# Unnormalised FFN inputs, an output projection traced in one go, and SSD running sums spread over the partitions by transfers

## The chip, the cores and the metric

The kernel runs on one core of a Trainium2 chip. The metric is the device time of one execution in microseconds (us); below, "before" is the kernel as it stood and "after" is the changed one. The core's engines are PE (TensorE, matrix multiply), DVE (VectorE), ACT (ScalarE), POOL (GpSimd) and SP (SyncE, which here only issues transfers). Each engine runs its own instructions in the order in which they stand in its program, and waits on semaphores for the others.

## The reference

Two layers of a hybrid decoder over a prompt of 512 tokens and eight sequences of eight new tokens each. Per layer:

```python
h = rmsnorm(x); u, z, xbc, dt, cq, ckv, kpe = split(h @ w_in)
y = concat(pool_mix(u), ssd_mix(z, xbc, dt), mla_mix(cq, ckv, kpe)) @ w_out
x = x + y
x = x + (relu(rmsnorm(x) @ w_up) ** 2) @ w_down     # rmsnorm: x * rsqrt(mean(x*x) + eps) * g
```

The SSD part takes chunks of 128 tokens. With `a = dt * A` per token and head, `a_cs = cumsum(a)` along the chunk, it needs the matrix `L[l, s] = exp(a_cs[l] - a_cs[s])` for s <= l, and `exp(a_cs[l])` for what comes in from the chunk before. One last rmsnorm gives the outputs.

## The kernel before

Activations lie transposed: 128 channels on the partitions, tokens along the free dimension. The tokens are worked on in two groups, c = 0 (256 prompt tokens) and c = 1 (256 prompt tokens and the 64 new ones, so 320 columns). Names carry layer, group and number: `out017` is the output projection of layer 0, group 1, output tile 7; `dn0033` is the down projection of layer 0, group 0, part 3, tile 3; `in102` is the input projection of layer 1, group 0, tile 2.

Every float32 product of a projection is three products of rounded parts (lines 201 to 203): weights and activations are split into a high part (`wh`, `gh`) and a low part (`wl`, `gl`). A weight tile comes in two halves of 256 KB (`wr`, line 177, issued by SP into four buffers); ACT makes `wh` (L191) and DVE `wl` (L192), in three buffers each, and a half feeds 12 matmuls. Results go to PSUM banks of tag `mm`, of which there are two.

The streams of work (input projection, SSD, attention over the prompt, attention of the new tokens, output projection, and the FFN of the other group) are generators, and a `Weave` takes steps from them in turn by rates. That gives the order in which instructions are traced, which is their priority. A scheduler of the framework then makes each engine's order from priorities and modelled times, so a change of a few lines moves instructions far from it.

Three places of this kernel matter here.

The input of the FFN: after the eight tiles of `w_out`, the sum of squares `ssf` is turned into `r` = rsqrt(mean) by a matmul with ones, then Ln and Exp on ACT (`rstd_of`). Then per tile DVE makes `fn` = x * g * r (L963), ACT the high part (L964), DVE the low part (L965). The splits are stored in the buffers that held the mixer's outputs, so they can begin once the last tile of `w_out` has read these. Only in layer 1, group 1 are the splits made without `r` (`late_norm`), and `r` is multiplied in after the up projection (L1016); elsewhere ACT applies Relu there (L1018).

The SSD's sums: `a` is split in two parts (`ah`, L816, L817) and per chunk b and head group g six matmuls with a column of it spread over all 128 columns put the running sums into a PSUM tile `rb` (L856), three heads side by side on every partition. ACT takes the exponential of it for `Ez` (L860), DVE adds the causal mask into `rm` (L863), ACT takes exp (L867), DVE multiplies by `cb` (L870), and PE uses it for `y` (L880). `rm` has two buffers.

The end: `finish_y` multiplies the eight tiles by r, two of them on POOL (L1030), and sends them out in pairs (L1032).

Of the kernel before, what the change touches and what calls it, by code (L numbers as in the profile page):

```python
# [9 lines left out]
F32 = mybir.dt.float32  # L10
F32R = mybir.dt.float32r
# [78 lines left out]
def step_kernel(ctx: ExitStack, tc: tile.TileContext, I, O):  # L90
# [121 lines left out]
    def rstd_of(c, ssum, n, name, tag):  # L212
# [6 lines left out]
        r = ap.tile([P, CM], F32, tag=tag, name=f"r_{name}", bufs=2)[:, :cw]  # L219
# [134 lines left out]
    def mixer(l, c, mp, ep):  # L354
# [252 lines left out]
        def sample_attn():  # L607
# [48 lines left out]
            ol = tr[0].tile([P, 6, NSEQ, DSEQ], F32, tag="ol", name=f"ol{l}{c}")  # L656
            for pq_ in range(NSEQ // 2):
# [72 lines left out]
                done.add(f"s{2 * pq_ + 1}")  # L730
                V.tensor_copy(ol[:, :, 2 * pq_:2 * pq_ + 2], po[:, :P].rearrange("p (u h t) -> p h u t", u=2, t=DSEQ)[:, :6])
# [36 lines left out]
        def ssd_dt():  # L768
# [46 lines left out]
            ah = mp.tile([P, 2, 18], F32R, tag="ah", name=f"ah{l}{c}")  # L815
            V.tensor_copy(ah[:, 0], a)  # L816
            V.tensor_tensor(ah[:, 1], a, ah[:, 0].bitcast(F32), op=ALU.subtract)  # L817
# [11 lines left out]
            st['dt'] = dt, ah, ncs, dec, tot  # L829
            yield 0.5  # L830

        def ssd():
            dt, ah, ncs, dec, tot = st['dt']
            for b in range(3 if smp_c else 2):
# [15 lines left out]
                for g in range(2):  # L850
                    r64 = slice(64 * g, 64 * g + 64)
                    rb = psum('sc', f"rb{l}{c}{b}{g}")
                    for r in range(3):
                        h = 3 * g + r
                        for i in range(2):
                            T.matmul(rb[:, r * n:r * n + n], ah[:n, i, 6 * b + h:6 * b + h + 1].broadcast_to([n, P]),  # L856
                                     CR('US')[:n] if smp else CR('U'), start=(i == 0), stop=(i == 1))
                    if not first:
                        ez = Ez[r64, g, :, :n]
                        A.activation(ez, rb[r64, :3 * n].rearrange("p (r k) -> p r k", r=3), AF.Exp)  # L860
                        V.tensor_tensor(ez, bc(xa[r64, 4, off:off + n], 3), ez, op=ALU.mult)
                    rm = mp.tile([P, 3, P], F32, tag="rm", name=f"rm{l}{c}{b}{g}", bufs=2)
                    V.tensor_tensor(rm[:n, :, :n], rb[:n, :3 * n].rearrange("p (r k) -> p r k", r=3),  # L863
                                    bc(C('mssds')[:n] if smp else C('mssd'), 3), op=ALU.add)
# [68 lines left out]
        def w_out():  # L933
# [6 lines left out]
            xu = []  # L940
            late_norm = l == DEPTH - 1 and c == 1
            for m in range(KT):
# [5 lines left out]
                if late_norm:  # L948
                    xu.append(t)
                sq_acc(c, ssf, t, m == 0, f"f{l}{c}{m}")  # L950
                yield 3.3
            if late_norm:
                ff[c] = act_tiles(c, f"f{l}{c}")
                for m in range(KT):
                    scaled_split(xu[m], ff[c], m, par(l, 'ffn_g', m))
                rf[0] = rstd_of(c, ssf, D, f"f{l}{c}", "rstd")
                return
            r = rstd_of(c, ssf, D, f"f{l}{c}", "rstd")
            ff[c] = act_tiles(c, f"f{l}{c}")
            for m in range(KT):  # L960
                pl, w_, tag, bufs = (ep, cw, "fn", 3) if c == 0 else (tr[0], 512, "ku", NK)
                t = pl.tile([P, w_], F32, tag=tag, name=f"fn{l}{c}{m}", bufs=bufs)[:, :cw]
# [38 lines left out]
    rf = [None]  # L1001
    NG, GT = 4, 8

    def ffn(l, c, fp, beside):
# [5 lines left out]
        def up(g, j):  # L1010
# [275 lines left out]
```

## Time and profile before

| | us |
|---|---|
| three runs, median (lowest to highest) | 1461.06 (1459.27 to 1461.63) |
| the profiled execution's own time | 1453.98 |
| its span, first to last instruction | 1452.2 |
| PE busy in it | 1405.4 (97%) |
| DVE busy | 1063.3 (73%) |
| ACT busy | 843.6 (58%) |

The profiled execution is one of the quicker ones: its own time lies 7.08 us under the median of the runs. A busy share is an average over the whole span. Where PE has work without a gap, time is the number of matmuls by their spacing; what the other engines do costs time only where PE waits for it. A matmul's own duration (some 0.3 us) is longer than its spacing, since matmuls are pipelined.

### The profile page before, as it was taken

Reading aid. Unit: us, or ns where it says so; the run is one execution under the profiler, and the core shown is the slowest. Engines: PE = TensorE matmul, PEld = TensorE weight load, DVE = VectorE, ACT = ScalarE, POOL = GpSimd, SP = SyncE. Lnnn points to the kernel's source line nnn. Section 1 sums busy time; section 2 is a strip of 40 time slices with the busy share of each in tenths; the row PEclk is TensorE's granted clock in tenths of the full one; section 3 lists DMA queues with packets and bytes.
Section 4 is the critical chain, followed back from the end, with each engine's and each line's share of the span. In section 5 each row is a group of like instructions: output and inputs, shape, how many; then the busy total and the mean of one; then the engine's idle time right before and its main releaser. Section 6 shows DMA issues by size and latency. Waiting matters only on the chain.

```text
span 1452.2 us, 30116 instructions
## 1 busy us (share of the span) xinstructions
PE 1405.4 (97%) x10552; PEld 1344.1 (93%) x10552; DVE 1063.3 (73%) x2353; ACT 843.6 (58%) x1781; POOL 74.7 (5%) x182
## 2 busy tenths in 40 slices
PE   7998989999999979999999999999999999999997
PEld 7968968999999979889999999899999999999997
DVE  6979769777666779856676679977777668675765
ACT  7756536665665657655454556656656666443444
POOL 0021013000000001100000001310000000000000
PEclk9999989999999999999999999999999999999999
DMA  7423416667545634434544553555675455444442
GB/s 230 132 70 123 142 41 210 196 205 239 161 144 177 201 114 141 139 103 154 162 151 154 167 165 122 157 195 168 209 233 169 130 175 170 151 151 148 153 150 105
DMA packets 152425, 228.95 MB, mean 158 GB/s; under 512 B 17874, under 2 KB 61010, under 8 KB 152274
## 3 DMA queue, kind: packets, MB, share of 16 engines
q1 hardware_dynamic: 138610, 216.69, 46.8%
q10 hardware_dynamic: 13664, 10.34, 2.3%
q8 instruction: 83, 1.36, 0.4%
q14 instruction: 68, 0.56, 0.1%
HBM read 219.32 MB, written 7.64 MB: 156 GB/s over the span
## 4 chain that ended last, share of the span: by engine, by line
PE 89%; DVE 5%; DMA 2%; ACT 2%; issue 1%; SPq 0%; ACTq 0%; DVEq 0%
PE dn L203 9%; PE dn L201 9%; PE dn L202 9%; PE up L203 9%; PE up L202 9%; PE up L201 9%; PE in L201 4%; PE in L203 4%; PE in L202 4%; PE out L201 2%; PE out L203 2%; PE out L202 2%; PE spo L726 2%; PE o L601 2%; PE rb L856 1%
## 5 line engine op out<-in xcount | busy, mean ns | idle before, releaser
L201 PE MATMUL up<-gh_f,wh_up 128*128 128x256 f32 (+1 forms) x1024 | 305.4, 299 | 1.8 <-ACT gh_f L238 1.1
L203 PE MATMUL up<-gh_f,wl_up 128*128 128x256 f32 (+1 forms) x1024 | 306.0, 300 | 0.1
L202 PE MATMUL up<-gl_f,wh_up 128*128 128x256 f32 (+1 forms) x1024 | 305.1, 298 | 0.3 <-DVE gl_f L239 0.3
L203 PE MATMUL dn<-hh,wl_dn 128*128 128x256 f32 (+1 forms) x1024 | 304.3, 298 | 0.6 <-DVE wl_dn L192 0.6
L201 PE MATMUL dn<-hh,wh_dn 128*128 128x256 f32 (+1 forms) x1024 | 303.4, 296 | 0.0
L202 PE MATMUL dn<-hl,wh_dn 128*128 128x256 f32 (+1 forms) x1024 | 303.0, 296 | 0.0
L191 ACT ACTIVATE wh_dn<-wr_dn 128x512 fp32r<-128x512 f32 x256 | 160.8, 631 | 185.7 <-PE dn L202 130.5
L191 ACT ACTIVATE wh_up<-wr_up 128x512 fp32r<-128x512 f32 x256 | 160.7, 629 | 165.7 <-PE up L202 108.4
L192 DVE TENSOR_TENSOR wl_dn<-wr_dn,wh_dn 128x512 fp32r<-128x512 f32 x256 | 176.4, 691 | 84.1 <-ACT wh_dn L191 76.8
L192 DVE TENSOR_TENSOR wl_up<-wr_up,wh_up 128x512 fp32r<-128x512 f32 x256 | 177.6, 696 | 63.1 <-ACT wh_up L191 55.3
L201 PEld LDWEIGHTS up<-gh_f,wh_up 128*128 128x128 f32 x1024 | 193.6, 189 | 4.2 <-ACT gh_f L238 1.3
L203 PEld LDWEIGHTS up<-gh_f,wl_up 128*128 128x128 f32 x1024 | 193.3, 189 | 4.6 <-DVE wl_up L192 1.6
L202 PEld LDWEIGHTS up<-gl_f,wh_up 128*128 128x128 f32 x1024 | 193.7, 189 | 1.9 <-issue 0.7
L203 PEld LDWEIGHTS dn<-hh,wl_dn 128*128 128x128 f32 x1024 | 192.8, 188 | 2.2 <-DVE wl_dn L192 1.0
L201 PEld LDWEIGHTS dn<-hh,wh_dn 128*128 128x128 f32 x1024 | 192.9, 188 | 1.4 <-issue 0.7
L202 PEld LDWEIGHTS dn<-hl,wh_dn 128*128 128x128 f32 x1024 | 192.8, 188 | 0.4 <-issue 0.2
L201 PE MATMUL in<-gh_h,wh_in 128*128 128x256 f32 (+3 forms) x448 | 137.7, 308 | 17.3 <-DVE cq L496 7.9
L203 PE MATMUL in<-gh_h,wl_in 128*128 128x256 f32 (+3 forms) x448 | 137.1, 306 | 1.5 <-DVE wl_in L192 1.5
L202 PE MATMUL in<-gl_h,wh_in 128*128 128x256 f32 (+3 forms) x448 | 137.2, 306 | 0.0
L201 PEld LDWEIGHTS in<-gh_h,wh_in 128*128 128x128 f32 (+1 forms) x448 | 84.9, 190 | 21.1 <-issue 8.3
L191 ACT ACTIVATE wh_in<-wr_in 128x512 fp32r<-128x512 f32 (+1 forms) x110 | 67.3, 614 | 61.3 <-PE in L202 49.5
L203 PEld LDWEIGHTS in<-gh_h,wl_in 128*128 128x128 f32 (+1 forms) x448 | 84.8, 189 | 4.0 <-DVE wl_in L192 2.2
(346 smaller groups left out, 2577.7 us busy)
## 6 DMA issues: line engine op xcount, KB each, us to landing
wr_up<-in_w_up SPq DMA_DIRECT2D x256, 256.0 KB, 2.8
wr_dn<-in_w_down SPq DMA_DIRECT2D x256, 256.0 KB, 2.9
wr_in<-in_w_in SPq DMA_DIRECT2D x110, 256.0 KB, 2.9
wr_out<-in_w_out SPq DMA_DIRECT2D x64, 256.0 KB, 2.9
ku<-in_kcache SPq DMA_DIRECT2D x96, 128.0 KB, 3.0
nat<-in_ncache SPq DMA_DIRECT2D x96, 64.0 KB, 2.0
ku<-in_kcache ACTq DMA_DIRECT2D x32, 128.0 KB, 3.1
wr_uq<-in_w_uq SPq DMA_DIRECT2D x12, 256.0 KB, 2.9
```

Source lines behind the costliest of these rows:

```text
L191: A.activation(hh, r, AF.Copy)
L192: V.tensor_tensor(ll, r, hh.bitcast(F32), op=ALU.subtract)
L201: T.matmul(ps[:mw, :cw], wh[:, kk, :mw], ah, start=(k == 0), stop=False)
L202: T.matmul(ps[:mw, :cw], wh[:, kk, :mw], al, start=False, stop=False)
L203: T.matmul(ps[:mw, :cw], wl[:, kk, :mw], ah, start=False, stop=(k == nk - 1))
L601: mark_pe[f"pa{l}{c}"] = T.matmul(po[64 * hh:64 * hh + 64, b * P:b * P + P], vT[i // 2][:, i % 2, h * 64:h * 64 + 64], pTs[hh][:, i * P:i ...
L726: mark_pe[f"s{l}{2 * pq_ + 1}"] = T.matmul(po[:, 64 * u:64 * u + NR], nat[:, g], pT[:, o_:o_ + NR], start=False, stop=True, skip_group_che ...
L856: T.matmul(rb[:, r * n:r * n + n], ah[:n, i, 6 * b + h:6 * b + h + 1].broadcast_to([n, P]), CR('US')[:n] if smp else CR('U'), start=(i == ...
```

## The change

FFN inputs: the path of `late_norm` becomes the only one. The splits are made from x * g alone (`scaled_split`: ACT L238, DVE L239 of before), r is kept per group (`rf`), and after the up projection DVE takes relu and r in one instruction; the second square moves from DVE to ACT. `w_out` of group 1 gets rate 5.0 in the weave instead of 1.0. SSD: the sums are made as rows (12 or 6 partitions by 128 or 64 tokens) by one more matmul per kind of chunk, copied to SBUF, written to DRAM (`crow`), and read back as a row spread over all 128 partitions, straight into `rm`, one transfer for each chunk and head group. `finish_y` no longer uses POOL.

```diff
-        r = ap.tile([P, CM], F32, tag=tag, name=f"r_{name}", bufs=2)[:, :cw]
+        r = ap.tile([P, cw if tag[:2] == 'rf' else CM], F32, tag=tag, name=f"r_{name}",
+                    bufs=2 if tag == 'rk' else 1)[:, :cw]
...
+                if ol is None:
+                    yield from need('ssd')
+                    ol = mp.tile([P, 6, NSEQ, DSEQ], F32, tag="rm", name=f"ol{l}{c}", bufs=2)
...
-            ah = mp.tile([P, 2, 18], F32R, tag="ah", name=f"ah{l}{c}")
-            V.tensor_copy(ah[:, 0], a)
-            V.tensor_tensor(ah[:, 1], a, ah[:, 0].bitcast(F32), op=ALU.subtract)
+            T.matmul(pc[:12, P:2 * P], a[:, :12], C('U'), start=True, stop=True)
+            if smp_c:
+                T.matmul(pc[:6, 2 * P:2 * P + CS], a[:CS, 12:18], C('US')[:CS], start=True, stop=True)
+            ct = mp.tile([12, P + CS], F32, tag="ct", name=f"ct{l}{c}")
+            A.activation(ct[:, :P], pc[:12, P:2 * P], AF.Copy)
+            crow = dram.tile([3, 6, P], F32, name=f"crow{l}{c}")
+            S.dma_start(crow[:2].rearrange("b h k -> (b h) k"), ct[:, :P])
+            if smp_c:
+                A.activation(ct[:6, P:], pc[:6, 2 * P:2 * P + CS], AF.Copy)
+                S.dma_start(crow[2, :, :CS], ct[:6, P:])
...
-                    rb = psum('sc', f"rb{l}{c}{b}{g}")
-                    for r in range(3):
-                        h = 3 * g + r
-                        for i in range(2):
-                            T.matmul(rb[:, r * n:r * n + n], ah[:n, i, 6 * b + h:6 * b + h + 1].broadcast_to([n, P]),
-                                     CR('US')[:n] if smp else CR('U'), start=(i == 0), stop=(i == 1))
+                    rm = mp.tile([P, 3, P], F32, tag="rm", name=f"rm{l}{c}{b}{g}", bufs=2)
+                    S.dma_start(rm[:, :, :n], crow[b, 3 * g:3 * g + 3, :n].unsqueeze(0).broadcast_to([P, 3, n]))
...
-            r = rstd_of(c, ssf, D, f"f{l}{c}", "rstd")
             ff[c] = act_tiles(c, f"f{l}{c}")
             for m in range(KT):
...
-                V.scalar_tensor_tensor(t, x[:, m, :cw], par(l, 'ffn_g', m), r, op0=ALU.mult, op1=ALU.mult)
-                A.activation(ff[c][0][:, m], t, AF.Copy)
-                V.tensor_tensor(ff[c][1][:, m], t, ff[c][0][:, m].bitcast(F32), op=ALU.subtract)
-                yield 0.0
+                scaled_split(x[:, m, :cw], ff[c], m, par(l, 'ffn_g', m))
+            rf[c] = rstd_of(c, ssf, D, f"f{l}{c}", f"rf{c}")
...
-            if rf[0] is not None and c == 1:
-                V.scalar_tensor_tensor(r, ps[:, :cw], 0.0, rf[0], op0=ALU.max, op1=ALU.mult)
-            else:
-                A.activation(r, ps[:, :cw], AF.Relu)
+            V.scalar_tensor_tensor(r, ps[:, :cw], 0.0, rf[c], op0=ALU.max, op1=ALU.mult)
...
-            V.tensor_tensor(r, r, r, op=ALU.mult)
+            A.activation(r, r, AF.Square)
...
-                    (G if k % 4 == 1 else V).tensor_tensor(x[:, k, :cw], x[:, k, :cw], r, op=ALU.mult)
+                    V.tensor_tensor(x[:, k, :cw], x[:, k, :cw], r, op=ALU.mult)
...
-                W.add(m1['w_out'], 1.0)
+                W.add(m1['w_out'], 5.0)
```

The change moves instructions on each engine. First DVE where layer 0 ends and layer 1 begins. Before, it finishes the FFN input of group 1 (`fn01`, `gl_f01`) right ahead of the first results of layer 1's input projection (`cq100` frees the PSUM bank of `in102`):

```order
L963 SCALAR_TENSOR_TENSOR fn016_7666<-x01_6908,prm0_73,r_f01_7637 128x320
L965 TENSOR_TENSOR gl_f01_7641<-fn015_7662,gh_f01_7640 128x320
L963 SCALAR_TENSOR_TENSOR fn017_7670<-x01_6908,prm0_73,r_f01_7637 128x320
L965 TENSOR_TENSOR gl_f01_7641<-fn016_7666,gh_f01_7640 128x320
L965 TENSOR_TENSOR gl_f01_7641<-fn017_7670,gh_f01_7640 128x320
L496 TENSOR_TENSOR cq100_7745<-in102_7720,r_in10_7698 128x256
L496 TENSOR_TENSOR cq101_7788<-in103_7763,r_in10_7698 128x256
```

Now the eight `gl_f01` stand among the down projections of group 0, between the two halves of the weight tile of `dn0033`:

```order
L192 TENSOR_TENSOR wl_dn0033_0_7372<-wr_dn0033_0_7369,wh_dn0033_0_7371 128x512
L240 SCALAR_TENSOR_TENSOR gl_f01_7303<-x01_6839,prm0_73,gh_f01_7302 128x320 x4
L1031 TENSOR_TENSOR x0_in_96<-x0_in_96,dn0032_7337 128x256
L240 SCALAR_TENSOR_TENSOR gl_f01_7303<-x01_6839,prm0_73,gh_f01_7302 128x320 x3
L231 TENSOR_TENSOR ssum_f01_6842<-ssum_f01_6842,sq_f017_7299 128x320
L240 SCALAR_TENSOR_TENSOR gl_f01_7303<-x01_6839,prm0_73,gh_f01_7302 128x320
L192 TENSOR_TENSOR wl_dn0033_4_7378<-wr_dn0033_4_7375,wh_dn0033_4_7377 128x512
```

So the work moved from ahead of layer 1's first evacuations to ahead of a low weight part of layer 0's last tiles. In the same way the eight `gl_f00` of group 0 now stand on DVE ahead of the second half of `in012`'s weights, in the middle of the computation of dt (`sm01`) of group 1:

```order
L240 SCALAR_TENSOR_TENSOR gl_f00_2870<-x0_in_96,prm0_73,gh_f00_2869 128x256 x5
L231 TENSOR_TENSOR ssum_f00_2305<-ssum_f00_2305,sq_f007_2839 128x256
L240 SCALAR_TENSOR_TENSOR gl_f00_2870<-x0_in_96,prm0_73,gh_f00_2869 128x256 x3
L792 TENSOR_SCALAR sm01_2728<-sm01_2728 128x18
L801 TENSOR_SCALAR sm01_2728<-sm01_2728 128x18
L192 TENSOR_TENSOR wl_in012_4_2986<-wr_in012_4_2983,wh_in012_4_2985 128x512
```

Before, these stood some sixty DVE instructions later, among the SSD of group 1. Next PE at the SSD of layer 0, group 1, from the sums (`cs01`) to the first result (`y010`). Before:

```order
L814 MATMUL cs01_2772<-sm01_2750,cst_77 64x6
L856 MATMUL rb0100_2807<-cu_78,ah01_2783 128x128
L856 MATMUL rb0101_2865<-cu_78,ah01_2783 128x128
L856 MATMUL rb0100_2807<-cu_78,ah01_2783 128x128 x5
L856 MATMUL rb0101_2865<-cu_78,ah01_2783 128x128 x5
L856 MATMUL rb0110_3000<-cu_78,ah01_2783 128x128 x6
L856 MATMUL rb0111_3017<-cu_78,ah01_2783 128x128 x6
L869 MATMUL cb0100_2821<-xaz01_1908 128x128
L869 MATMUL cb0101_2879<-xaz01_1908 128x128
L880 MATMUL y010_2882<-rm0100_2816,xd010_2801 64x128
```

And now:

```order
L818 MATMUL cs01_2750<-sm01_2728,cst_77 64x6
L819 MATMUL cs01_2750<-cu_78,sm01_2728 12x128
L821 MATMUL cs01_2750<-cu_78,sm01_2728 6x64
L874 MATMUL cb0100_2798<-xaz01_1886 128x128
L874 MATMUL cb0101_2850<-xaz01_1886 128x128
L885 MATMUL y010_2853<-rm0100_2790,xd010_2784 64x128
```

The 24 matmuls between `cs01` and `cb0100` are gone, two have come, and `y010` follows directly. The transfers that `y010` now needs stand on SP, all eight in a row, ahead of the first weights of the FFN:

```order
L177 DMA wr_in0110_4_3345<-in_w_in 128x512
L825 DMA crow01_2765<-ct01_2763 12x128
L828 DMA crow01_2765<-ct01_2763 6x64
L864 DMA rm0100_2790<-crow01_2765 128x384
L864 DMA rm0101_2842<-crow01_2765 128x384
L864 DMA rm0110_2955<-crow01_2765 128x384
L864 DMA rm0111_2966<-crow01_2765 128x384
L864 DMA rm0120_3126<-crow01_2765 128x3x64
L864 DMA rm0121_3151<-crow01_2765 128x3x64
L177 DMA wr_up0000_0_3450<-in_w_up 128x512
```

Before, `wr_up0000_0` followed `wr_in0110_4` at once.

## Rows read from the trace of the kernel before

**Rows 1.** The page: span, and busy time of the engines.

```profile
span 1452.2 us, 30116 instructions
...
PE 1405.4 (97%) x10552; PEld 1344.1 (93%) x10552; DVE 1063.3 (73%) x2353; ACT 843.6 (58%) x1781; POOL 74.7 (5%) x182
```

**Rows 2.** Waits of PE: who waited for whom, total us, times, longest.

```profile
PE in L201 <- DVE cq L496: 7.9, 1, 7.9
...
PE cb L869 <- ACT bt L848: 3.2, 2, 2.1
```

**Rows 3.** The chain that ended last, 516 to 525 us: start, us, what.

```profile
516.18 0.55 DVE fn L963
...
523.51 0.50 DVE gl_f L965
...
524.61 0.46 PE in L201
```

**Rows 4.** Windows: length; busy us of PE, PEld, DVE, ACT, POOL; PEclk, DMA share, GB/s.

```profile
175.00:210.00 35.00, 28.59 (x182) 23.32 (x183) 25.51 (x70) 16.85 (x49) 2.04 (x5) 0.76 0.10 31
...
525.00:530.00 5.00, 5.00 (x30) 5.00 (x29) 2.90 (x7) 2.26 (x6) 0.00 (x0) 0.63 0.14 40
...
650.00:850.00 200.00, 200.00 (x1400) 199.95 (x1399) 131.81 (x239) 105.00 (x197) 1.46 (x6) 1.00 0.50 161
850.00:1000.00 150.00, 149.99 (x1193) 138.85 (x1192) 128.10 (x316) 91.70 (x200) 26.57 (x50) 1.00 0.50 159
```

**Rows 5.** Groups by line and form: the split on DVE, 256 and 320 columns.

```profile
L239 DVE SCALAR_TENSOR_TENSOR gl_h<-x_in,prm,gh_h 128x256 fp32r<-128x256 f32 x16 | 7.5, 479 | 0.5 <-ACT gh_h L238 0.5
...
L239 DVE SCALAR_TENSOR_TENSOR gl_h<-x,prm,gh_h 128x320 fp32r<-128x320 f32 x8 | 4.4, 546 | 0.0
```

**Rows 6.** The chain that ended last: matmuls of L856 in three stages.

```profile
52.64 0.62 PE rb L856 x6
...
551.69 1.29 PE rb L856 x12
...
881.88 1.07 PE rb L856 x10
```

**Rows 7.** DVE and SP in order of time: weight parts at 167 us, weight loads.

```profile
166.65 0.68 DVE L192 TENSOR_TENSOR wl_in<-wr_in,wh_in 128x512 fp32r<-128x512 f32 x1
...
167.74 0.68 DVE L192 TENSOR_TENSOR wl_in<-wr_in,wh_in 128x512 fp32r<-128x512 f32 x1
...
44.02 0.80 SPq L177 DMA_DIRECT2D wr_in<-in_w_in  x2
...
206.68 6.26 SPq L177 DMA_DIRECT2D wr_up<-in_w_up  x3
```

**Rows 8.** PE in order of time, SSD of layer 0, group 1.

```profile
175.06 0.39 PE L801 MATMUL cs<-sm,cu 128*128 128x12 f32 x2 [0.67 <-DVE sm L799]
...
176.65 2.40 PE L856 MATMUL rb<-cu,ah 128*128 128x128 f32 x12
...
183.92 0.70 PE L880 MATMUL y<-rm,xd 128*64 128x128 f32 x4 [0.64 <-DVE rm L870]
...
195.50 0.70 PE L880 MATMUL y<-rm,xd 128*64 128x128 f32 x4 [1.20 <-DVE rm L870]
```

**Rows 9.** Transfers: KB each, median us from issue to landing.

```profile
nat<-in_ncache SPq DMA_DIRECT2D x96, 64.0 KB, 2.0
...
h<-in_state_ssm SPq DMA_DIRECT2D x8, 192.0 KB, 2.7
...
pw<-in_pool_w SPq DMA_DIRECT2D x2, 128.0 KB, 5.8
```

**Rows 10.** Groups by line and form: after the up projection, on DVE.

```profile
L1016 DVE SCALAR_TENSOR_TENSOR fr<-up,r_f 128x320 f32<-128x320 f32 x32 | 15.6, 491 | 14.9 <-PE up L203 14.9
...
L1022 DVE TENSOR_TENSOR fr<-fr 128x320 f32<-128x320 f32 x64 | 31.2, 489 | 3.1 <-ACT hh L1021 0.4
```

**Rows 11.** Line 1030 after 1400 us: ns min/median/max, first and last start.

```profile
L1030 DVE TENSOR_TENSOR x<-x,r_y x6: 477/485/1145, 1444.1 to 1447.5; 128x320 f32<-128x320 f32 x6
L1030 POOL TENSOR_TENSOR x<-x,r_y x2: 1098/1130/1162, 1444.2 to 1445.3; 128x320 f32<-128x320 f32 x2
```

More of the change, by code (lines that the diff above doesn't have):

```diff
@@ L655, in sample_attn @@
             V.tensor_copy(ckt, tp[:CS, :P])
-            ol = tr[0].tile([P, 6, NSEQ, DSEQ], F32, tag="ol", name=f"ol{l}{c}")
+            ol = None
             for pq_ in range(NSEQ // 2):
@@ L828, in ssd_dt @@
             A.activation(tot[:, :NT6], pc[:, 24:24 + NT6], AF.Exp)
-            st['dt'] = dt, ah, ncs, dec, tot
+            st['dt'] = dt, crow, ncs, dec, tot
             yield 0.5
         def ssd():
-            dt, ah, ncs, dec, tot = st['dt']
+            dt, crow, ncs, dec, tot = st['dt']
             for b in range(3 if smp_c else 2):
@@ L851, in ssd @@
                     r64 = slice(64 * g, 64 * g + 64)
-                    rb = psum('sc', f"rb{l}{c}{b}{g}")
-                    for r in range(3):
-                        h = 3 * g + r
-                        for i in range(2):
-                            T.matmul(rb[:, r * n:r * n + n], ah[:n, i, 6 * b + h:6 * b + h + 1].broadcast_to([n, P]),
-                                     CR('US')[:n] if smp else CR('U'), start=(i == 0), stop=(i == 1))
+                    rm = mp.tile([P, 3, P], F32, tag="rm", name=f"rm{l}{c}{b}{g}", bufs=2)
+                    S.dma_start(rm[:, :, :n], crow[b, 3 * g:3 * g + 3, :n].unsqueeze(0).broadcast_to([P, 3, n]))
                     if not first:
                         ez = Ez[r64, g, :, :n]
-                        A.activation(ez, rb[r64, :3 * n].rearrange("p (r k) -> p r k", r=3), AF.Exp)
+                        A.activation(ez, rm[r64, :, :n], AF.Exp)
                         V.tensor_tensor(ez, bc(xa[r64, 4, off:off + n], 3), ez, op=ALU.mult)
-                    rm = mp.tile([P, 3, P], F32, tag="rm", name=f"rm{l}{c}{b}{g}", bufs=2)
-                    V.tensor_tensor(rm[:n, :, :n], rb[:n, :3 * n].rearrange("p (r k) -> p r k", r=3),
-                                    bc(C('mssds')[:n] if smp else C('mssd'), 3), op=ALU.add)
+                    V.tensor_tensor(rm[:n, :, :n], rm[:n, :, :n], bc(C('mssds')[:n] if smp else C('mssd'), 3), op=ALU.add)
                     for r in range(3):
@@ L939, in w_out @@
             ssf = ssum_tile(c, f"f{l}{c}")
-            xu = []
-            late_norm = l == DEPTH - 1 and c == 1
             for m in range(KT):
@@ L1000, in step_kernel @@
     ff = [None, None]
-    rf = [None]
+    rf = [None, None]
     NG, GT = 4, 8
@@ L1029, in finish_y @@
                 for k in range(KT):
-                    (G if k % 4 == 1 else V).tensor_tensor(x[:, k, :cw], x[:, k, :cw], r, op=ALU.mult)
+                    V.tensor_tensor(x[:, k, :cw], x[:, k, :cw], r, op=ALU.mult)
                     if k % 2:
-                        (A if c == 0 else S).dma_start(O[f'o_y{c}'][:, k - 1:k + 1], x[:, k - 1:k + 1, :cw])
+                        (A if c == 0 or k % 4 == 1 else S).dma_start(O[f'o_y{c}'][:, k - 1:k + 1], x[:, k - 1:k + 1, :cw])
         def down(g, m):
```

10 lines of the change are left out of this document (removed).

## The prediction

> **What bounds the kernel now.** I read the page first. PE is busy for 1405.4 of 1452.2 us [rows 1], so the bound is the length of PE's own work, and only 47 us of idle time can be won elsewhere. Hence two questions: which matmuls does the change remove where PE has no gap, and which of PE's waits go or come?
>
> The list of PE's waits answers the second. Its longest single entry is one matmul of an input projection that waits 7.9 us for DVE's `cq` [rows 2]. The chain of waits shows why: where layer 0 passes into layer 1, DVE makes the FFN input of group 1 without a break from 516.18 to 524.01, and only then the `cq` that frees a PSUM bank [rows 3]. [...] The weak stretch is 175 to 210, the SSD of layer 0's group 1: 28.59 busy of 35 us at a clock of 0.76, because there is no other work to put beside the chain from the sums to `y`.
>
> **The change part by part.** All sums are against the profiled execution, 1453.98 us, of which the span is 1452.2.
>
> *The wait at the layer boundary.* `fn` goes, and the splits no longer wait for r; they stand with the down projections, far ahead of `cq100`. What remains in front of `cq100` is the r of layer 1 itself: about 0.5 us of wait is left (an estimate: one ones-matmul, two ACT steps and one DVE step against 14 matmuls of cover). So 7.9 - 0.5 = 7.4 us go. The slow clock goes with the wait: a mean of 0.63 over 5 us means that 3.7 us ran at half speed, 1.85 us lost [rows 4]. Together -9.25.
>
> What is late instead is the weight half behind the burst. Eight splits of 320 columns at 546 ns [rows 5] and two other DVE instructions of about 0.5 make some 5.3 us, then 0.7 for the weight part itself: 6 us between two halves. PE holds at most three halves of 12 matmuls, at 200 us / 1400 = 0.143 each [rows 4], 5.1 us. A stall of about 1 to 2 us: +1.5, between 0 (the splits come quicker than modelled here) and 4. Net -7.75. In layer 1 the same burst existed already for group 1 and only moves; for group 0 it lies beside 320-column tiles, whose three halves cover 8 x 0.48 us. Both at 0.
>
> *The matmuls of L856.* Layer 1 group 0: 12 of them last 1.29 us in the chain [rows 6], so 24 take 2.6, and PE has no gap there to fill. Group 1: 24 more at the same pace (1.07 for 10) 2.6, and 12 of 64 columns, between nothing and the price of the wide ones, 1.3: I take 0.8. Layer 1 thus gives 2.6 + 3.4 = 6.0. Layer 0 group 0: four times 0.62, 2.5 us. Six row matmuls come; no row shows one of them, bounded by 0 and by two of L856 for each (0.2): I take the upper end, +1.
>
> *The transfers.* They stand on SP, and SP waits at each until its source is there, with everything behind it waiting too. In layer 1 the weight loads behind them wait for free buffers anyway, so 0. In layer 0 group 0, two loads that went out at 44.02 [rows 7] now wait behind a write of a few KB (2.0 us, by the 64 KB transfers of [rows 9]) and two more issues (0.4 each, by the same two loads): about 3 us late. I charge 2.5, between 0 (other matmuls stand in front) and 4; it eats the 2.5 us of L856 there. In group 1 of layer 0 the FFN weights behind the eight transfers went out only at 206.68 [rows 7], later than the last of these can be issued: 0.
>
> *The SSD of layer 0, group 1.* Here PE does not set the time, the chain does, so the 36 matmuls that go give nothing by themselves. First, the `gl_f00` burst now stands between the two halves of `in012`: they were 1.1 us apart (166.65 and 167.74) [rows 7], and are now 1.1 + 8 x 0.48 = 4.9 apart, of which 12 matmuls cover 1.7: the sums come about 3 us later, at 178. From there, before: 1.6 us to the first L856, 2.4 for twelve of them, 4.9 from their end to `y` [rows 8]. Now: 1.6 + 0.4 for two row matmuls, 0.3 for the copy (estimate), a write of 2.0, a read of 192 KB at 2.7 and 0.4 for the second one's issue [rows 7, 9], then the same 4.9: `y` at 190.4 instead of 183.92, 6.5 late. Second chunk: before, 11.6 us from `y` to `y` (183.92, 195.50) [rows 8], with sixteen FFN instructions of DVE in between; now some 3 us of `y` until `rm` is free, 2.7 + 0.4 for the row, and 4.4 for the chain behind it (4.9 less what is done while the row is under way, an estimate): 10.5, so 5.4 late. Then it comes back: PE's 3.2 us of waits for `cb` [rows 2] lose their cause, since work of the input projection now stands in front of the third chunk, and its 12 matmuls of L856 at the low clock are saved (about 1.2 us by the half pace of rows 6). +1 net, between -4 (the DVE relief counts in full) and +9 (nothing comes back, and the low clock lasts).
>
> *What I cost at nothing.* In the FFN, DVE swaps a square for the relu-and-scale (489 against 491 ns at 320 columns) [rows 10]; ACT swaps a Relu for a Square; PE is busy for 200 of 200 us beside it [rows 4], so no cover is lost. `w_out` in one go changes the order of matmuls, not their number. At the end, DVE does eight multiplications instead of six with two on POOL. One of the six took 1145 ns, where the median is 485, while POOL ran [rows 11]: 5 x 0.485 + 1.145 = 3.6 against 8 x 0.485 = 3.9, so +0.3 at most, and I leave it at 0. [...]
>
> *Sum:* -7.75 - 6.0 + 1 - 2.5 + 2.5 + 1 = -11.75, so 1442.2 us for the profiled execution. The median of the runs before is 1461.06, 7.08 above its profiled execution; I carry the difference over: 1461.06 - 11.75 = 1449.3, about 1449.
>
> **The rivals.** *A, the transfers decide (slower).* Each of the three rounds in the SSD of layer 0 group 1 (first rows, second chunk, third chunk) is a transfer that PE waits for in order. For it: 128 partitions read the same row of DRAM, which no row here shows, and 128 KB have taken 5.8 us [rows 9]. At 5.8 instead of 2.7, three rounds cost 9.3 more, the low clock over the longer stretch some 5 (0.76 now), and in layer 0 group 0 and layer 1, four more chunks wait 2 each: +22, that is +10, 1471; at half of that price 1460. It decides from a landing time of about 4.5 us on, where the sum crosses zero. Against it: the 5.8 was measured at the start, under the load of the first weights, and the stretch here has next to no traffic (a DMA share of 0.10 in 175 to 210 [rows 4]). [...]
>
> *B, the boundary gives little back.* The wait moves to the next cause: the weight half behind the burst (up to 4), or r of layer 1. Then -9.25 becomes about -4, the SSD of layer 0 costs +4, and the sum is -3: 1458. For it: two PSUM banks alone carry the projections. Against it: the order has four whole down projections of 24 matmuls between the burst and `cq100`.
>
> *C, more comes.* The DVE relief in 186 to 200 counts in full (-4 instead of +1), the weights of layer 0 group 0 are not late (0 instead of +2.5) and the burst costs nothing: -20.75, 1440.
>
> **How the numbers follow.** Forecast (-6 to -18, 1443 to 1455): 0.68. C: 0.08. B: 0.14. A: 0.10. What a measurement can tell from no change is 0.2%, 2.9 us. Of B half is a gain above that; the rest, and a tenth of A, is no change: faster 0.68 + 0.08 + 0.07 = 0.83, same 0.08, slower 0.09. The range runs from C's 1440 to the half-priced A, 1460; what lies past it is most of A and a part of C.
>
> **What would show it.** Right: PE's list of waits without the 7.9 us for `cq`, and a clock of 1.0 in the window after the boundary; the matmuls of L856 gone, and the stretches of layer 1's SSD still without gaps; row transfers that land in 2 to 3 us; `y` of layer 0 group 1 some 6 us later after its sums than the 8.9 of now, with the FFN's start no later. Wrong: a wait of PE for `rm` of more than 5 us in one piece, SP waiting on the row write while a weight tile is missing, or a stall of over 4 us behind one of the bursts.

## The result and the profile after

The changed kernel is slower: 1476.72 us in the median (1475.31 to 1479.87, four runs) against 1461.28 (1459.27 to 1461.63, four runs) beside it. The ratio is 1.0124 with a 95% interval of 1.0099 to 1.0150, so some 18 us more (14 to 22; the two medians lie 15 us apart, and sizes below go by the ratios). The forecast was 1449 with a range of 1440 to 1460: wrong in sign and outside the range.

The traces differ by more than the runs, 1478.1 against 1452.2 us of span, since the profiled execution of before lies 7 us under its median and that of after 3 over it. The places are read from the traces, the sizes of whole edits from the runs.

The busy times of after (they answer to [rows 1]):

```profile
span 1478.1 us, 30077 instructions
...
PE 1411.3 (95%) x10444; PEld 1344.7 (91%) x10444; DVE 1046.3 (71%) x2293; ACT 867.8 (59%) x1819; POOL 66.7 (5%) x178
```

PE executes fewer matmuls and is still busy for 5.9 us longer; its idle time rose from 46.8 (1452.2 - 1405.4) to 66.8. The mean granted clock, of before and then of after (core, span, clock), tells why it is busy for longer:

```profile
core 0: 1452.2 us, clock 0.988
```

```profile
core 0: 1478.1 us, clock 0.975
```

A mean of 0.988 over 1452.2 us means 17.4 us of full speed lost; 0.975 over 1478.1 means 37.0. So there are two costs, 20 us more of waiting and some 20 more of lost speed, less the matmuls that went. The rest of this text uses "lost speed" for this product. Waiting and lost speed overlap, since the mean clock covers idle time too: in 188 to 200 us, shown below, PE is busy for 5.36 of 12 us at 0.57.

PE's waits of after (sum, times, longest; they answer to [rows 2]):

```profile
PE y L885 <- DVE rm L875: 8.8, 3, 6.3
PE cb L874 <- ACT bt L859: 5.7, 4, 2.0
...
PE y L897 <- DMA h<-in_state_ssm: 4.4, 3, 2.6
PE sc L581 <- ACT kT L549: 3.2, 1, 3.2
```

The list of before has these two as well, next to [rows 2]:

```profile
PE in L201 <- ACT se L419: 3.4, 1, 3.4
...
PE y L880 <- DVE rm L870: 1.8, 2, 1.2
```

The 7.9 us for `cq` is gone, as forecast. The waits for the rows' product `rm` rose from 1.8 to 8.8 us and those for `bt` (on ACT) from 3.2 to 5.7. New are the waits for `kT` (also on ACT) and for the sample states `h`, which no list of before has.

Where the lag arose, by the start of the DVE split of the same weight tile (us later than in before, own time of before in the second column; the version without rows is told of below):

| weight tile, place | before | after | after, L856 kept and no rows |
|---|---|---|---|
| `in007`, as the SSD of layer 0 group 0 begins | 43 | -0.1 | 0.2 |
| `in0111`, after that SSD | 117 | +8.9 | 0.2 |
| `in011`, group 1's projection | 161 | +7.8 | 0.9 |
| `in012`, second half, behind the burst of splits | 168 | +11.0 | 4.1 |
| `up0001`, after the first chunks of group 1 | 228 | +2.9 | 1.5 |
| `up0003`, in its sample chunk | 237 | +13.8 | 0.8 |
| `in102`, second half, before the layer boundary | 509 | +20.9 | 4.8 |
| `in104`, after it | 537 | +11.7 | -5.4 |
| `up0103`, second half, after the SSD of layer 1 group 0 | 595 | +16.9 | -4.9 |
| `in118`, before that of group 1 | 880 | +18.0 | -4.0 |
| `dn1002`, after it | 967 | +25.8 | -1.7 |

As a whole every SSD stage loses, and only the boundary gains. The lags hold the difference between the two executions as well as that of the kernels, since the one of before was quick. The windows of after (length, busy and count by engine, then clock, DMA share and GB/s) show what the stages look like. Those of layer 0 answer to the 175 to 210 us of [rows 4], and the last two, the SSD of layer 1 group 1, to its 150 us without a gap:

```profile
86.00:98.00 12.00, 9.33 (x56) 6.77 (x56) 7.81 (x22) 5.43 (x19) 1.57 (x7) 0.72 0.24 79
...
104.00:111.00 7.00, 5.73 (x13) 3.20 (x13) 3.14 (x9) 3.00 (x10) 0.00 (x0) 0.51 0.01 2
188.00:200.00 12.00, 5.36 (x30) 3.97 (x30) 3.73 (x8) 4.01 (x12) 0.00 (x0) 0.57 0.21 60
...
232.00:248.00 16.00, 14.91 (x104) 12.49 (x105) 8.03 (x20) 4.75 (x12) 6.96 (x14) 0.57 0.35 105
...
500.00:545.00 45.00, 43.49 (x336) 42.10 (x335) 36.15 (x75) 29.58 (x63) 0.00 (x0) 1.00 0.58 175
...
890.00:950.00 60.00, 55.42 (x381) 50.98 (x379) 53.63 (x127) 35.28 (x84) 15.26 (x38) 0.97 0.42 130
950.00:1000.00 50.00, 46.01 (x420) 41.33 (x419) 37.51 (x89) 27.44 (x64) 7.40 (x12) 0.93 0.53 164
```

Before, the stretch that corresponds to the first two ran at a clock of 1.00 though PE idled there as well, and so did the 40 us behind the 3.4 us for `se`, which lie in the third line:

```profile
85.00:102.00 17.00, 14.71 (x88) 9.96 (x88) 11.97 (x38) 9.57 (x29) 2.28 (x9) 1.00 0.17 57
102.00:122.00 20.00, 17.61 (x104) 14.36 (x103) 15.11 (x41) 11.82 (x29) 3.57 (x10) 1.00 0.16 54
...
120.00:124.00 4.00, 0.74 (x6) 0.47 (x4) 3.93 (x10) 1.21 (x3) 0.47 (x3) 1.00 0.23 75
122.00:162.00 40.00, 37.53 (x288) 37.00 (x288) 33.12 (x74) 23.56 (x48) 1.98 (x9) 1.00 0.48 154
```

In the window from 232 to 248 of after PE is busy for 14.91 of 16 us at a clock of 0.57: a wait of 2.6 us for `h` stands ahead of it, and the lower clock behind it costs more than the wait (0.43 of 16 us, some 7, an estimate). Not every wait is followed by a lower clock: behind the 3.4 us for `se` it stayed at 1.00. The window from 500 to 545 has the boundary in it: a clock of 1.00, and 1.5 us idle in 45.

One wait in full, from the chain of after in the SSD of layer 1 group 0 (start, duration, what):

```profile
562.80 0.33 PE cs L819 x2
563.15 0.28 ACT ct L823
563.44 1.88 DMA crow<-ct
565.34 3.63 DMA rm<-crow
568.99 0.57 DVE rm L869
...
569.88 0.68 ACT rm L872 x2
570.56 0.52 ACT wh_in L191
571.08 0.28 ACT kT L549
571.40 0.55 PE sc L581 x2
```

The two transfers take 5.5 us one after the other. ACT's exponential (L872) needs the row, by way of DVE's mask (L869), and ACT stands idle for 3.07 us in front of it. Behind it on ACT stand the weight half `wh_in` and `kT`, which have nothing to do with the SSD, and PE waits 3.2 us for `kT`. Over the whole trace (the tile `rm` of after: issue, who waited, landing):

```profile
L864 SPq DMA_DIRECT2D rm<-crow x20: 319/381/1218, 45.9 to 957.2; - x20
...
ACT Ez L867: 24.9, 15
...
DMA to landing us min/median/max: 2.9/3.6/4.6
```

And SP's queue in layer 0 group 1 (start, duration from first to last issue, times); it answers to the loads of [rows 7], where the first FFN weight went out at 206.68:

```profile
189.35 22.68 SPq L864 DMA_DIRECT2D rm<-crow  x6
212.80 0.35 SPq L177 DMA_DIRECT2D wr_up<-in_w_up  x1
...
229.49 0.33 SPq L892 DMA_DIRECT2D h<-in_state_ssm  x1
```

The six reads hold SP for 22.7 us, since four of them wait until `rm` is free. The state that PE then waits for goes out at 229.49; in before this load went out at 216.91. The hold is not needed to make the two loads late, though. With the rows issued from POOL (experiment 2) neither goes out sooner:

```profile
212.85 15.76 SPq L177 DMA_DIRECT2D wr_up<-in_w_up  x5
...
230.24 0.33 SPq L892 DMA_DIRECT2D h<-in_state_ssm  x1
```

What is late is the sample chunk itself. Its first product with a state starts on PE at 212.4 us before, at 221.9 in after and at 221.5 with the rows from POOL, and SP's load of a state waits until an earlier state has been sent out (8.6 us in three waits in after).

### The profile page after: what moved, and what is told of

It is laid out like the page before. It is cut to its first block, busy times and chain, and to the rows that moved or that the text cites. A ratio compares the mean times of both kernels' runs of the same rounds, so it can differ in the third digit from the quotient of the medians.

```text
span 1478.1 us, 30077 instructions
## 1 busy us (share of the span) xinstructions
PE 1411.3 (95%) x10444; PEld 1344.7 (91%) x10444; DVE 1046.3 (71%) x2293; ACT 867.8 (59%) x1819; POOL 66.7 (5%) x178
## 4 chain that ended last, share of the span: by engine, by line
PE 83%; DVE 6%; DMA 4%; ACT 3%; issue 2%; SPq 0%; ACTq 0%; POOL 0%; DVEq 0%
PE dn L203 9%; PE dn L201 9%; PE dn L202 9%; PE up L201 9%; PE up L203 9%; PE up L202 9%; PE in L201 3%; PE in L203 3%; PE in L202 3%; PE out L201 2%; PE out L203 2%; PE out L202 2%; PE spo L727 2%; PE o L602 1%; DMA rm<-crow 1%
## 5 line engine op out<-in xcount | busy, mean ns | idle before, releaser
L201 PE MATMUL up<-gh_f,wh_up 128*128 128x256 f32 (+1 forms) x1024 | 310.0, 303 | 2.9 <-DVE fr L1005 2.1
L203 PE MATMUL up<-gh_f,wl_up 128*128 128x256 f32 (+1 forms) x1024 | 311.6, 305 | 0.6 <-DVE wl_up L192 0.6
L202 PE MATMUL up<-gl_f,wh_up 128*128 128x256 f32 (+1 forms) x1024 | 308.5, 301 | 0.0
L201 PEld LDWEIGHTS up<-gh_f,wh_up 128*128 128x128 f32 x1024 | 198.1, 193 | 6.4 <-DVE fr L1005 2.4
L203 PEld LDWEIGHTS up<-gh_f,wl_up 128*128 128x128 f32 x1024 | 198.0, 193 | 3.2 <-DVE wl_up L192 1.0
L202 PEld LDWEIGHTS up<-gl_f,wh_up 128*128 128x128 f32 x1024 | 197.9, 193 | 1.6 <-issue 1.3
L201 PE MATMUL in<-gh_h,wh_in 128*128 128x256 f32 (+3 forms) x448 | 137.8, 308 | 10.3 <-ACT gh_h L239 4.9
L1005 DVE SCALAR_TENSOR_TENSOR fr<-up,r_f 128x320 f32<-128x320 f32 (+1 forms) x128 | 58.3, 456 | 47.2 <-PE up L203 46.8
```

Source lines behind the costliest of these rows:

```text
L201: T.matmul(ps[:mw, :cw], wh[:, kk, :mw], ah, start=(k == 0), stop=False)
L202: T.matmul(ps[:mw, :cw], wh[:, kk, :mw], al, start=False, stop=False)
L203: T.matmul(ps[:mw, :cw], wl[:, kk, :mw], ah, start=False, stop=(k == nk - 1))
L1005: V.scalar_tensor_tensor(r, ps[:, :cw], 0.0, rf[c], op0=ALU.max, op1=ALU.mult)
```

## The experiments

Times are medians; the ratio to the kernel before, run beside each, follows with its interval, and where two versions are compared the ratios are, taken on 1458 us.

**1. The two halves of the change apart.** The FFN part alone: the hunks of `rstd_of`, `w_out`'s splits, `rf` and `up`, with `ol` in the tag `rm`. The SSD part alone: the hunks of the sums, `crow` and `rm`. And the change without its SSD part.

```diff
# FFN part alone, on before
+                scaled_split(x[:, m, :cw], ff[c], m, par(l, 'ffn_g', m))
...
+            rf[c] = rstd_of(c, ssf, D, f"f{l}{c}", f"rf{c}")
...
+            V.scalar_tensor_tensor(r, ps[:, :cw], 0.0, rf[c], op0=ALU.max, op1=ALU.mult)
# SSD part alone, on before
+            S.dma_start(crow[:2].rearrange("b h k -> (b h) k"), ct[:, :P])
...
+                    S.dma_start(rm[:, :, :n], crow[b, 3 * g:3 * g + 3, :n].unsqueeze(0).broadcast_to([P, 3, n]))
```

> The kernel before with the FFN part of the change alone: unnormalised FFN inputs, r applied behind the up projection, the second square on ScalarE, and `ol` in the tag `rm` (without that the tiles don't fit); the matmuls of L856 stay. Theory (the row transfers cost the time, the FFN part gives the 9 us of the boundary that were forecast): faster by 6 to 10 us, 1451 to 1455, with the wait for `cq` gone from PE's list. Rival 1 (the boundary gives nothing back, or the bursts of splits cost it): within 3 us of before, 1458 to 1464, or slower. Rival 2 (the outputs in one go are to blame): as the theory here.

> The kernel before with the SSD part alone: sums as rows, written to DRAM and spread by transfers; FFN and output projection as before. The lags by stage, read between the two traces, are about 8 us in the SSD of layer 0 group 0, 11 in group 1, 6 and 8 in layer 1. Theory: slower by 20 to 30 us, 1481 to 1491. Rival 2 (output projection in one go, or the new order, is to blame): slower by less than 8 us, under 1469.

> The changed kernel with the matmuls of L856 put back in place of the row transfers; FFN inputs, output projection in one go and the end of the kernel as changed. Theory: as the FFN part alone within 3 us, 1450 to 1456. Rival 2 (the output projection in one go costs): slower than the FFN part alone by 8 us or more, 1460 or above.

Measured: FFN part 1452.94, 0.9957 (0.9935 to 0.9979); SSD part 1476.94, 1.0129 (1.0106 to 1.0152); the change without its SSD part 1452.86, 0.9966 (0.9943 to 0.9988). So the FFN part gives 6 us, the SSD part costs 19, and the outputs in one go and the end cost nothing that can be told. The two halves make -6 + 19 = 13 us (8 to 17 by their intervals), short of the 18 (14 to 22) of the whole, but the intervals overlap. Rival 2 (the outputs in one go) falls. The SSD part fell just short of the 20 expected.

**2. SP's queue or the transfers.** The changed kernel, with write and reads issued from POOL.

```diff
-            S.dma_start(crow[:2].rearrange("b h k -> (b h) k"), ct[:, :P])
+            G.dma_start(crow[:2].rearrange("b h k -> (b h) k"), ct[:, :P])
...
-                    S.dma_start(rm[:, :, :n], ...
+                    G.dma_start(rm[:, :, :n], ...
```

> The changed kernel with the row write and the row reads issued from POOL's queue instead of SP's, so that no weight load waits behind them. If SP being held is what costs (weights and states late), it comes down to 1455 to 1465. If the chain of two transfers itself costs (PE waits for rm whoever issues it), it stays within 5 us of the changed kernel, 1471 to 1481, with the same waits of PE for `rm` at y.

Measured: 1465.48, 1.0046 (1.0030 to 1.0063): 11 us better than the changed kernel, 12 worse than without rows. It lies between the two expectations. The landing is no quicker (3.7 us in the median against 3.6) and an issue takes longer (557 ns in the median, against SP's 381):

```profile
L864 POOL DMA_DIRECT2D rm<-crow x20: 539/557/781, 48.6 to 939.4; - x20
```

What is saved is thus neither landing nor issue. That leaves the waiting in front of the issues, with what stood behind it on SP, or the order, which moved too; no run separates the two. In the traces half of the gain falls into layer 0 (a lag of 3.3 instead of 11.7 at `in104`) and most of the rest into the SSD of layer 1 group 0, where the lag falls by 1.5 instead of rising by 5.2 and the 3.2 us for `kT` are gone. The SSD of layer 1 group 1 still loses 7.4.

**3. The rows asked for earlier.** Both reads of a chunk are issued ahead of its transposes, then 4 us of other streams' steps; from SP, and from POOL.

```diff
+                rms = []
+                for g in range(2):
+                    rm = mp.tile([P, 3, P], F32, tag="rm", ...)
+                    S.dma_start(rm[:, :, :n], ...)          # or G.
+                    rms.append(rm)
+                yield 4.0
                 px = psum("tp", f"px{l}{c}{b}")
```

> The changed kernel with both row reads of a chunk issued ahead of the chunk's transposes and some 4 us of other streams' work put between the issue and the first use. In the changed kernel ScalarE stood 24.9 us in 15 waits in front of the exponentials that read the rows (L867), with everything behind them on its queue waiting too. Theory (an in-order engine that waits for the rows is what costs): most of those 24.9 us go, below 5, and the time falls by 8 to 15 us, to 1462 to 1469. Rival (the held queue of SP, weights and states late): ScalarE's wait falls too but the time stays within 4 us of 1477.

> The same, with the row write and reads issued from POOL's queue instead of SP's. The two remedies act on two causes: POOL's queue alone took 11 us off. Theory (both causes): 1450 to 1458, near the 1453 of the version that keeps the matmuls of L856, a little under it if the removed matmuls are worth anything. Rival (one cause only): no better than the better of the two remedies alone, 1465.

Measured: SP 1456.41, 0.9995 (0.9977 to 1.0013); POOL 1444.38, 0.9914 (0.9890 to 0.9938). The times fell further than expected, but not for the reason given: from SP, ACT still waits 23.5 us in 14 waits for the rows, though 19 us of time are gone. The sum of ACT's waits is thus no price; it is likely that one costs only where something that PE needs stands behind it. The lead had also moved the chunk in the order, and whether that or the covered transfer was the gain needed a control.

**4. The control: the same lead without any transfer.** On the version without rows.

```diff
+                yield 4.0
                 px = psum("tp", f"px{l}{c}{b}")
```

> The version with the matmuls of L856 and no transfers (1453), with the same 4 us of other streams' work put ahead of each chunk's transposes as in the version with the early row reads. If that version gained because its transfers were covered, this changes nothing here: 1450 to 1457. If it gained because the chunk stands elsewhere in the order, whatever feeds it: faster, 1440 to 1447.

Measured: 1441.56, 0.9898 (0.9871 to 0.9925). My theory of the covered transfer falls: the lead is worth 10 us with the old matmuls too, by where it puts the chunk. Its median is the lowest of all versions, some 15 us under before, and it has no row transfers. (The interval of the version with rows from POOL overlaps with its own.) Four more versions fill in the table, with leads of 2 and 8 us (each edit as above with another number), and a fifth is the kernel before with the lead of 4 us.

> The early row reads on POOL's queue with a lead of 8 us of other streams' work instead of 4. If a transfer of 3.5 us is covered with 4 already: the same within 3 us, 1441 to 1447. If the lead is still too short (13 waits for the rows, 15.9 us, are left): faster by 4 us or more.

> The version without transfers (matmuls of L856 kept) with a lead of 2 us ahead of each chunk's transposes; without a lead 1453, with 4 us 1441.6. If the gain of the lead is a trend (chunk further from its inputs): between the two, 1444 to 1452. If it is an accident of one order: outside.

> The same with a lead of 8 us. The version with row reads on POOL's queue and that lead took 1451.4. If the rows are worth their removed matmuls once they are covered (8.5 us, the prediction's term): this one is slower than 1451.4 by 5 or more, 1456 or above. If the rows cost a few us in any order: 1441 to 1450.

> Row reads on POOL's queue with a lead of 2 us. Rows on POOL against no rows stood at +12.6 us without a lead and at +2.8 with 4 us. If the transfer's latency is what is left, it should lie between, 3 to 12 us above the version without rows and the same lead. If only the order counts, it can lie on either side of it.

> The kernel before with nothing changed but the lead of 4 us ahead of each chunk's transposes. If the lead is worth its 11 us whatever else is changed: 1444 to 1450. If it needs the FFN inputs as changed: 1455 to 1462.

| lead | L856, no rows | rows from POOL | rows from SP |
|---|---|---|---|
| none | 1452.9, 0.9966 | 1465.5, 1.0046 | 1476.7, 1.0124 |
| 2 us | 1450.7, 0.9955 (0.9938 to 0.9973) | 1465.1, 1.0056 (1.0039 to 1.0074) | not run |
| 4 us | 1441.6, 0.9898 | 1444.4, 0.9914 | 1456.4, 0.9995 |
| 8 us | 1446.4, 0.9912 (0.9878 to 0.9946) | 1451.4, 0.9964 (0.9947 to 0.9982) | not run |

The lead on the kernel before: 1448.59, 0.9935 (0.9913 to 0.9957). So the lead is worth some 9 us by itself, and needs nothing of the change. Rows issued by SP instead of POOL cost 11 and 12 us in the two orders where both ran. Rows from POOL against no rows cost 12, 15, 2 and 8 us: dearer in each order, though at 4 us the intervals overlap; the 15 us lie past the 3 to 12 expected of a latency that is left over. A longer lead does not cover more: at 8 us the version with rows got 7 us slower, against both of its expectations. Since every one of these edits also moves hundreds of instructions, the sign, the same in four orders and clear in three of them, is firmer than any single entry.

**5. What the removed matmuls are worth.** With rows, the matmuls of L856 done as well (result unused); without rows, each of them done twice.

```diff
# rows kept, L856 added back
+                    rb = psum('sc', f"rb{l}{c}{b}{g}")
+                    for r in range(3):
+                        h = 3 * g + r
+                        for i in range(2):
+                            T.matmul(rb[:, r * n:r * n + n], ah[...].broadcast_to([n, P]), ...)
```

> The changed kernel, rows and transfers as they are, with the matmuls of L856 done as well in their old place; nothing reads their result. If PE has no time to spare there, as the prediction had it, they cost what was booked as a gain, 8.5 us: 1485. If PE waits there anyway, they cost nothing: 1474 to 1480. If what costs is the lower clock behind gaps that these matmuls had filled, it is faster than the changed kernel: 1465 to 1473.

> The version with the matmuls of L856 (rows left out, the rest of the change as it is; 1453) with each of these matmuls done twice. If one set is worth 8.5 us as the prediction had it: 1460 to 1463. If they lie where PE waits anyway: 1452 to 1456.

Measured: 1463.06, 1.0031 (1.0006 to 1.0057), 14 us faster than the changed kernel with more work in it; and 1473.12, 1.0093 (1.0064 to 1.0123), 19 us slower than one set. Both lie outside all that was expected. The first speaks for matmuls that fill a gap, the second against matmuls that lie in one; in both the rest of the order moved too (in the first the exponentials of the second chunk stand three weight halves earlier on ACT). As a price for L856 both are inconclusive. The first does price the transfers with nothing removed: with the matmuls in both, 1.0031 against 0.9966 is some 9 us (4 to 14), again with another order. The price of the matmuls is better read between the two versions with a lead of 4 us. Span and clock, then busy times, without rows:

```profile
core 0: 1437.9 us, clock 0.992
```

```profile
PE 1398.4 (97%) x10552; PEld 1340.5 (93%) x10552; DVE 1039.7 (72%) x2301; ACT 867.9 (60%) x1813; POOL 67.1 (5%) x178
```

and with rows from POOL:

```profile
core 0: 1441.8 us, clock 0.990
```

```profile
PE 1391.0 (96%) x10444; PEld 1329.3 (92%) x10444; DVE 1040.0 (72%) x2293; ACT 865.7 (60%) x1819; POOL 86.3 (6%) x204
```

Busy falls by 7.4 us while 2.9 more of speed is lost (14.4 against 11.5). If PE had been at work wherever the clock was low, the matmuls would be worth 7.4 + 2.9 = 10.3 at full clock. With rows it was not, in the longest such stretch:

```profile
177.00:194.06 17.06, 11.41 (x46) 7.55 (x46) 5.70 (x14) 6.72 (x20) 2.72 (x5) 0.50 0.17 46
```

So the matmuls are worth between 7.4 and 10.3 us, an estimate. Idle time rises from 39.5 to 50.8, by 11.3. In these two executions the removal is real, and the waiting for what replaced it takes it all back.

**6. The clock behind the waits.** The changed kernel with 40 matmuls more (the profile counts 80, 10524 against 10444), in three places where PE waited. The last ten share a PSUM bank with sums of the sample chunk, and a part of group 1's outputs is another.

```diff
+                for _ in range({(0, 0, 1): 8, (0, 1, 0): 22}.get((l, c, b), 0)):
+                    T.matmul(py[:64, 384:], xd[:, 0], ones, start=True, stop=True)
...
+                        for _ in range(10 if (l, f) == (0, 1) else 0):
+                            T.matmul(py[:, 384:], bm, ones[:CS], start=True, stop=True)
```

> The changed kernel with 40 matmuls added whose result nothing reads, in three places where PE waited: 8 ahead of the second chunk's y in layer 0 group 0 (a wait of 2.3 us), 22 ahead of the first y in layer 0 group 1 (6.3), 10 ahead of the third pair of sample states (2.6). Behind these waits the granted clock was at its lower level from 90 to 98, from 189 to 200 and from 233 to 248 us. Theory (what follows a wait costs as much as the wait: PE at half speed): these stretches go in whole or in large part, and the kernel with more work is faster by 6 to 13 us, 1464 to 1471. Rival (the waits alone cost, the clock nothing that these matmuls can give back): 1475 to 1482.

Measured: 1470.30, 1.0086 (1.0052 to 1.0121): about 6 us faster than the changed kernel, at the low end of what was expected, but the intervals overlap. The windows of the changed kernel over the three places, then those of this version, and its mean clock:

```profile
84.00:112.00 28.00, 21.74 (x101) 14.83 (x100) 15.98 (x44) 13.76 (x42) 3.37 (x11) 0.76 0.14 46
180.00:212.00 32.00, 21.26 (x140) 16.55 (x139) 18.91 (x56) 15.28 (x42) 0.00 (x0) 0.79 0.28 83
226.00:250.00 24.00, 21.42 (x146) 17.54 (x145) 15.21 (x36) 7.94 (x19) 11.34 (x24) 0.72 0.37 114
```

```profile
84.00:112.00 28.00, 23.72 (x130) 15.76 (x128) 16.64 (x48) 15.54 (x47) 2.84 (x10) 0.88 0.11 39
180.00:212.00 32.00, 26.00 (x182) 20.46 (x180) 19.14 (x52) 14.51 (x42) 0.12 (x1) 0.89 0.25 74
226.00:250.00 24.00, 23.96 (x193) 21.04 (x193) 15.82 (x35) 12.82 (x30) 10.20 (x22) 0.91 0.47 143
```

```profile
core 0: 1467.5 us, clock 0.984
```

23.5 us of speed are lost instead of 37.0. The clock is clear of noise, 0.981 to 0.987 in the four runs against 0.975 to 0.978 in the four of the changed kernel. So the slow stretches go in part when PE has something to do in the waits; that the time falls with them is likely and not shown.

**7. The write ahead of the read.** The reads take a table in DRAM instead of `crow`. It is written once at the start and holds -1000 for every sum, so this version leaves the real sums out of what it computes from the rows.

```diff
-                    S.dma_start(rm[:, :, :n], crow[b, 3 * g:3 * g + 3, :n].unsqueeze(0).broadcast_to([P, 3, n]))
+                    S.dma_start(rm[:, :, :n], stat[0][:, :n].unsqueeze(0).broadcast_to([P, 3, n]))
```

> The changed kernel with the row reads taken from a table in DRAM that is written once at the start (all sums read as -1000), so that no read waits for the write of the sums; the writes are still made and SP still waits for a free `rm`. If the write ahead of the read is the larger part of the cost: down by 10 us or more, below 1467. If the read alone leaves PE waiting: 1468 to 1477.

Measured: 1472.79, 1.0105 (1.0082 to 1.0128). By the ratios some 3 us of the cost are the wait for the write, and since the intervals overlap it may be none. The trace says more: PE's wait for the rows' product at `y`, 8.8 us in after, is no longer in the list, and PE waits on ACT instead (first fence). ACT itself waits for the rows as long as in after, 25.4 us against 24.9 (second fence).

```profile
PE cb L874 <- ACT bt L859: 8.1, 5, 3.7
...
PE cb L874 <- ACT tot L839: 3.2, 1, 3.2
```

```profile
ACT Ez L867: 25.4, 14
```

The reads, the wait of SP for a free `rm` and the order are left for the rest; no run separates them.

## Why the prediction was wrong

*The boundary: right.* Forecast -9.25; the lag falls from 20.9 to 11.7, by 9.2, and the same step of the FFN part alone is 8.3 (7.4 to -0.9). The +1.5 for the weight half behind the burst can't have been more: PE idles for 1.5 us in all from 500 to 545 of after. Rival B, by which the boundary was to give little back, falls with it. Behind the 7.9 us for `cq` the clock of before (length, PE busy and count, clock, DMA share, GB/s) was 0.50 and soon after 1.00:

```profile
525.00:528.00 3.00, 3.00 (x16) 0.50 0.15 43
...
531.00:534.00 3.00, 3.00 (x26) 1.00 0.35 98
```

Matmuls of 256 columns start 0.21 us apart in the first and 0.12 apart in the second. There are 18 at the wider spacing, from 524.61 to 528.49, which lose some 1.6 us (18 x 0.09, an estimate) where 1.85 was forecast. In after, the window from 500 to 545 has 1.00.

*The burst ahead of `in012`: right.* The half came 3.2 us late (7.8 to 11.0; forecast 3). In the FFN part alone the lag goes from 2.7 to 5.8 there, to 1.9 by 206 us and to 6.3 by `up0001`, so what became of it is open. The FFN part as a whole gave 6 us where -7.75 was forecast for the boundary and its burst.

*"The matmuls of L856": the size right, the use wrong.* Forecast 8.5 of matmuls gone less 1 for the new ones; by experiment 5 it is 7.4 to 10.3 of PE time. The step then took this time off the end because "PE has no gap there to fill". That was true of layer 1 in the kernel before [rows 4]. With the rows the chunk's `y` waits for two transfers in series, and PE has gaps that it did not have: 8.6 us idle in the 110 from 890 to 1000.

*"The transfers": the step that failed.* It priced them at 0 in layer 1 and +2.5 in layer 0 group 0. Together with the gain of the matmuls, the forecast for these stages was thus -6.0 and 0. Measured in the trace: +5.2 and +7.8 in layer 1, +8.9 in layer 0 group 0; in the runs the rows in place of the matmuls cost 23 us from SP and 12 from POOL. The step looked at one queue, SP's, and in layer 1 at its weights alone. Three things were left out, and how the cost divides among them no run shows:
- ACT reads the row first (16 of the 20 rows; DVE the other four), and waits for it in order: 24.9 us in 15 waits, with `kT`, `bt` and weight halves behind it. The prediction had named SP as the engine that waits, and asked of no other what stands behind it. One such wait leads to PE's 3.2 us for `kT`; the sum is no price (experiment 3).
- SP waits for a free `rm` too, up to 5.2 us in one wait, and not for the write alone. Issuing from POOL took off 11 us; in layer 0 group 1, where SP was held longest, the loads behind went out no sooner for it.
- In after, waits of 2.3, 6.3 and 2.6 us in layer 0 go with stretches at a mean clock of 0.72, 0.57 and 0.57. The prediction counted such a loss at the boundary alone, and as 5 us in rival A.

*The SSD of layer 0 group 1: the chain was right, the rest was not.* From the sums to `y` 12.3 us were forecast; the start of `y` less that of the first sum, in the timeline of PE, gives 11.3:

```profile
184.34 0.39 PE L805 MATMUL cs<-sm,cu 128*128 128x12 f32 x2
...
195.61 0.70 PE L885 MATMUL y<-rm,xd 128*64 128x128 f32 x4 [6.26 <-DVE rm L875]
```

That is 2.4 us more than before; the "some 6 us later after its sums" of the prediction's list of signs does not follow from its own 12.3. By `up0001` the lag was indeed down to 2.9. Then the sample chunk, with its late states and a clock of 0.57 (232 to 248 us), added 10.9 (2.9 to 13.8). The stage as a whole cost 6.0 (7.8 to 13.8), inside the +1's bounds of -4 and +9, but not for the reasons given: the waits for `cb`, 3.2 us before, were to lose their cause and came to 4.1 here (1.9 for `bt`, 1.8 for `tot`, 0.4 for `hz`), and the FFN's weights started at 212.80 instead of 206.68.

*The signs.* Of those named for a wrong prediction the first came: one wait for `rm` of 6.3 us, where more than 5 was the mark. Of those for a right one, `cq` and the clock at the boundary came, and layer 1 without gaps and reads that land in 2 to 3 us did not.

*What was costed at nothing: one line misread.* Of the six multiplications on DVE two, not one, were long beside POOL (1141 and 1145 ns), and without POOL all eight are short (482 to 491 ns):

```profile
L1030 DVE TENSOR_TENSOR x<-x,r_y x2: 1141/1143/1145, 1444.5 to 1445.6; 128x320 f32<-128x320 f32 x2
...
L1017 DVE TENSOR_TENSOR x<-x,r_y x8: 482/484/491, 1471.6 to 1474.4; 128x320 f32<-128x320 f32 x8
```

From the first start to the last end the six took 3.8 us and the eight take 3.3, where +0.3 was the bound.

*Rival A had the sign and not the mechanism.* It was to decide from a landing of about 4.5 us; the median was 3.6 (the prediction took 2.7) and the kernel was slower all the same. The argument against it, that the stretch has next to no traffic, settled nothing: the reads landed between 2.9 and 4.6 us, none of them as fast as the 2.7.

Left open: some 7 us of lag between 237 and 509 us, in the attention of the new tokens, were not followed up (the version without rows gains 4.0 there too), and how much of a single entry of the table is the accident of one order was not separated.

## What to carry over

Before work on the bound engine (the one that sets the time, here PE) is traded for a transfer, list every engine that will wait for it in order (here ACT first, then DVE, SP for the free buffer), and write down what stands behind each wait; a transfer is "hidden" only if all of these are. Price a wait of the bound engine with the slower clock that can follow it (a mean of 0.57 to 0.72 in three stretches of after). And when an edit gains, run its placement alone: here a lead of 4 us, without any of the rest, gave 9 us on the old kernel, and the version with the lowest median keeps the matmuls.

## What was not expected of the hardware

A kernel with 40 matmuls more lost 13.5 us less of speed and was not slower for them (some 6 us faster, with intervals that overlap). Waits of 2.3 to 6.3 us went with a clock of 0.57 to 0.72 in after, while one of 3.4 us in before left it at 1.00. The same row read landed no quicker from POOL (3.7 us in the median, against 3.6 from SP) and was issued more slowly (557 against 381 ns), and the version was still 11 us faster.
